# Recurrence heads in two parts, a banded pair that stays on the chip, and gates two ahead: a fused transformer kernel on one core

## The chip, the cores and the metric

The kernel runs on one core of one Trainium2 chip. The metric is the device time of one execution in microseconds (us); the number before is the median of three runs. The engines are named as in the profile: PE is TensorE (matmuls), PEld its weight loads, DVE is VectorE, ACT is ScalarE, POOL is GpSimd, SP is SyncE, which issues the transfers here.

## The reference, cut to what matters

A first block (gated delta mixer, then a convolutional gated feed-forward) is followed by two layers of a second block on 512 positions of width 1024. All of the change lies in the second block:

```python
for l in range(2):
    h = rmsnorm(x, g_mix[l])
    (a_cq, a_ckv, a_kr, b_q, b_ff, b_fb, b_i, b_g, c_q, c_k, c_v,
     gate_a, gate_b, gate_c) = split_cols(h @ w_in[l])
    y_a = mla(a_cq, a_ckv, a_kr, ...)          # low-rank attention, 8 heads
    y_b = hgrn2(b_q, b_ff, b_fb, b_i, b_g, ..) # gated recurrence, 8 heads, forward and backward
    y_c = window_gqa(c_q, c_k, c_v, ...)       # banded attention, 8 heads, blocks of 128
    merged = (sigmoid(gate_a) * (y_a @ w_br_a[l]) + sigmoid(gate_b) * (y_b @ w_br_b[l])
              + sigmoid(gate_c) * (y_c @ w_br_c[l]))
    x = x + merged @ w_out[l]
    x = x + cross(rmsnorm(x, g_x[l]), ...)
    x = x + swiglu(rmsnorm(x, g_ffn[l]), ...)
```

## The kernel before, in words

Everything is fp32, made of products of a rounded high part and a low rest: a matrix product is three matmuls per 128 rows (`mm3`, L158 to L160). A **strip** (`strip`) is one 128-column block of `h @ w_in`: 24 matmuls of 128x512 into one PSUM bank, behind one weight load (SP), one cast to the high part (`cast_hi`, L111, on ACT) and one subtraction for the low part (`sub_lo`, L120, on DVE, on POOL for the early gates). The weights have three raw buffers and two each of high and low parts; strips have three PSUM banks (`psg`), scores and the recurrence's triangles two (`psa`), transposes and states two (`psb`), outputs one (`pso`).

`layer` runs, in the order of the text: `hgrn`, `mla`, `branch` b, `window`, `branch` a, `branch` c, the output projection, `cross`, `ffn`. The text's order isn't the queues' order. A planner plays the program ahead of the run with its own model of times and fills each engine's queue; of the instructions that it holds ready it takes the one that stands first in the text, and `high_priority(100)` moves a block 100 places forward. So an engine runs later work where earlier work isn't ready, as far as buffers allow. What is planned is fixed: on the chip every engine works through its queue in order.

A recurrence head (`hgrn_head`) has two halves. **Strips and gates** (to L1069): three strips (q, forward and backward gate), and for each direction a chain over ACT, DVE and POOL (exponentials, a scan at L1048, products at L1045, L1053, L1054, L1055), then the block decays `XE` (L1062 to L1069). **Products** (from L1071): level and block tiles (L1084, L1095 on DVE and POOL), 16x16 up to 64x64 triangles on PE (L1107 to L1121), transposes (L1129), the state chain (L1148 on PE, L1151 on ACT or L1153 on DVE, six steps in turn in one bank), and the output matmuls (L1158). Even and odd heads have separate pools for the tiles of the gates; the tiles of the products (`hlv`, `hbk`, `hkm`, `hkt`, `hA`) are shared. `hgrn` calls the heads one after the other; at odd heads it first makes the strip of the output gate, and after each head `early_gate` makes one strip of the branch gates with its sigmoid and stores it for later (8 of them here, 8 more in `mla`, which serve branches b and a).

`mla` starts with loads of the rotary tables `cos`, `sin`, `ssin` into its pool `low`, two strips for the key rank and three for the query rank, each followed by a norm, and then, in a block with `high_priority(AHEAD)`, AHEAD being 100, the strip of the rotary key (evacuated at L797 and L798) and the value product (L814 to L816). Its pools lie where those of `hgrn` lay.

`window` works four pairs of heads (s = 0 to 3); each pair's output `Y` goes to DRAM (`keep_y`, L737) and `branch_in` (L1179 to L1181) loads it back (`yl`, L99) and splits it into `ys`. `branch` then makes, for each of eight blocks m, the gate (loaded if early, else a strip and a sigmoid, which holds for branch c alone) and the product of 12 matmuls with the `ys` of its four pairs.

Of the kernel before, what the change touches and what calls it, by code (L numbers as in the profile page):

```python
# [9 lines left out]
F32R = mybir.dt.float32r  # L10
BF16 = mybir.dt.bfloat16
I32 = mybir.dt.int32
AF = mybir.ActivationFunctionType
# [4 lines left out]
P = 128  # L18
# [6 lines left out]
def f32(ap):  # L25
    return ap.bitcast(F32)
# [631 lines left out]
def c2(p, name):  # L658
    o, n = p.cst2_off[name]
    return p.c2[:, o:o + n]  # L660
# [74 lines left out]
def keep_y(p, y, ys):  # L735
    d = p.dram([P, 512], "yd")
    p.nc.sync.dma_start(d, y)  # L737
    ys.append(d)


def side_by_side(p, ps, out, scale=None):
# [16 lines left out]
def mla(p, l, G, low, mid, high):  # L758
# [9 lines left out]
            acc = p.square_add(acc, z[i], i == n - 1)  # L768
        return z, p.rstd_rows(acc, nf)


    cos, sin, ssin = (p.load(p.ins["big"][i], n, 1, pool=low) for n, i in (("cos", 0), ("sin", 1), ("ssin", 2)))
    z, rr = rank(at["ckv"], 2, 256, "za")
    CKV = []
    for i in range(2):
# [5 lines left out]
    nc.vector.tensor_scalar(g, p.col(f"a_gq{l}"), 96 ** -0.5, None, MULT)  # L781
    CQ = [p.split(z[i], "CQ", 6, g[:, i:i + 1], pool=low) for i in range(3)]

    def four():
        t = p.t("s4", 4, 1024)
        return t[:, :512], t[:, 512:]
# [2 lines left out]

    half = (slice(0, 64), slice(64, 128))  # L790
    kh, kl = ([p.t(f"{n}{i}", 1, dtype=F32R) for i in range(2)] for n in ("kh", "kl"))

    V = []
    with p.tc.high_priority(AHEAD):
        ps = p.strip(w_in, at["kr"], p.X)
        a, b = four()
        nc.vector.tensor_tensor(a[:64], ps[:64], cos[:64], MULT)  # L797
        nc.vector.tensor_tensor(b[:64], ps[64:], ssin[:64], MULT)  # L798
        nc.gpsimd.tensor_tensor(a[:64], a[:64], b[:64], ADD)
        nc.gpsimd.tensor_tensor(a[:64], a[:64], p.r[:64], MULT)  # L800
        for i in range(2):
            R = half[1 - i]
            m = c2(p, "keven")[:64, i:i + 1]
            nc.scalar.activation(kh[i][R], a[:64], AF.Identity, scale=m)
            nc.vector.scalar_tensor_tensor(kl[i][R], a[:64], m, f32(kh[i][R]), MULT, SUB)

        wvh, wvl = p.wload(f"w_uv{l}", 0, 1024)
        for t in range(4):
            ps = p.ps()
            ts = slice(t * P, t * P + P)  # L810
            for k in range(2):
                xh, xl = CKV[k]
                c = slice(k * 512, k * 512 + 512)
                nc.tensor.matmul(ps, xh[:, ts], wvh[:, c], start=k == 0, stop=False)  # L814
                nc.tensor.matmul(ps, xh[:, ts], wvl[:, c], start=False, stop=False)
                nc.tensor.matmul(ps, xl[:, ts], wvh[:, c], start=False, stop=k == 1)  # L816
            V.append(side_by_side(p, ps, p.t("V", 4, 1024, F32R)))

    nc.vector.tensor_tensor(cos, cos, rq, MULT)
    nc.gpsimd.tensor_tensor(sin, sin, rq, MULT)  # L820
# [66 lines left out]
def window(p, l, G):  # L887
    nc = p.nc
    at = G.at
    w_in = f"w_in{l}"  # L890
    half = [slice(0, 64), slice(64, 128)]


    k = strip_r(p, w_in, at["ck"])
    K = []
    for kv in range(2):
        kh, kl = p.t("K", 2, dtype=F32R), p.t("Kl", 2, dtype=F32R)
        for i in range(2):
            nc.scalar.activation(kh[half[i]], k[half[kv]], AF.Copy)
        nc.vector.tensor_tensor(kl[half[kv]], k[half[kv]], f32(kh[half[kv]]), SUB)  # L900
        nc.gpsimd.memset(f32(kl[half[1 - kv]]), 0.0)
        K.append((kh, kl))
    v = strip_r(p, w_in, at["cv"])
    pv = p.ps("b")
    for t in range(4):
        nc.tensor.transpose(pv[:, t * P:t * P + P], v[:, t * P:t * P + P], p.ident)

    V = []
    for kv in range(2):
        t = p.t("V", 2)  # L910
        c = lambda a, i: a.rearrange("p (t i c) -> p t i c", t=4, i=2)[:, :, i]
        nc.scalar.copy(c(t, kv), c(pv, kv))
        nc.gpsimd.memset(c(t, 1 - kv), 0.0)
        V.append(t)
    for s in range(4):
        q = strip_r(p, w_in, at["cq2"] + s)
        O = p.ps("o")
        Y = p.t("x", 3, keep=True)
        T = {}
        for kv in range(2):  # L920
            h = s + 4 * kv
            R = slice(kv * 64, kv * 64 + 64)
            qq = p.t("Q", 8, dtype=F32R)
            nc.scalar.activation(qq[R], q[R], AF.Copy)
            nc.gpsimd.tensor_tensor(qq[half[1 - kv]], q[R], f32(qq[R]), SUB)
            kh, kl = K[kv]
            sink = p.col(f"sink{l}")[:, h:h + 1]
            wb = window_bias_head(p, h)
            negm, den, es = (p.small([P, 4], n, 3) for n in ("w4m", "w4d", "w4e"))
            E = []  # L930
            for qb in range(4):
                k0, k1 = max(qb - 1, 0), min(qb + 2, 4)
                W = (k1 - k0) * P
                qs = slice(qb * P, qb * P + P)
                ks = slice(k0 * P, k1 * P)
                sc = p.ps("a")[:, :W]
                nc.tensor.matmul(sc, qq[:, qs], kh[:, ks], start=True, stop=False)
                nc.tensor.matmul(sc, qq[:, qs], kl[:, ks], start=False, stop=True)
                sb = p.t("wsb", 10, 384)[:, :W]
                off = (k0 - qb + 1) * P  # L940
                nc.vector.tensor_tensor_reduce(sb, sc, wb[:, off:off + W], 0.125, sink, ADD, MAX,
                                               accum_out=negm[:, qb:qb + 1])
                nc.vector.tensor_scalar(negm[:, qb:qb + 1], negm[:, qb:qb + 1], -1.0, None, MULT)
                nc.scalar.activation(sb, sb, AF.Exp, bias=negm[:, qb:qb + 1], accum_out=den[:, qb:qb + 1])
                E.append(sb)
            nc.scalar.activation(es, negm, AF.Exp, bias=sink)
            nc.vector.tensor_tensor(den, den, es, ADD)
            nc.vector.reciprocal(den, den)
            for qb in range(4):
                k0, k1 = max(qb - 1, 0), min(qb + 2, 4)  # L950
                W = (k1 - k0) * P
                qs = slice(qb * P, qb * P + P)
                nc.vector.tensor_scalar(E[qb], E[qb], den[:, qb:qb + 1], None, MULT)
                pt = p.ps("b")[:, :W]
                for kb in range(k1 - k0):
                    nc.tensor.transpose(pt[:, kb * P:kb * P + P], E[qb][:, kb * P:kb * P + P], p.ident)
                pts = p.t("pts", 8, 384)[:, :W]
                nc.scalar.copy(pts, pt)
                T[kv, qb] = pts
                if kv == 1:  # L960
                    for i in range(2):
                        for kb in range(k0, k1):
                            nc.tensor.matmul(O[:, qs], V[i][:, kb * P:kb * P + P],
                                             T[i, qb][:, (kb - k0) * P:(kb - k0) * P + P],
                                             start=i == 0 and kb == k0, stop=i == 1 and kb == k1 - 1)
        nc.scalar.copy(Y, O)
        keep_y(p, Y, G.y["c"])

# [13 lines left out]
def hgrn(p, l, G, pools, tail):  # L984
# [8 lines left out]
    for t in range(4):  # L993
        V.append(p.t("Vb", 4))
        nc.scalar.activation(V[t], pst[t], AF.Identity, scale=p.rc[:, t:t + 1])
    for h in range(8):
        if h % 2 == 0:
            O = p.ps("o")
        else:
            z = strip_r(p, w_in, at["bg"] + h // 2)  # L1000
            a = p.sigmoid(z, p.t("za", 3, keep=True))
            nc.gpsimd.tensor_tensor(a, z, a, MULT)
        hgrn_head(p, l, G, h, V, O[(h % 2) * 64:(h % 2) * 64 + 64], pools[h % 2])
        early_gate(p, l, G)
        if h % 2 == 1:
            o = p.t("x", 3, keep=True)
# [8 lines left out]
            keep_y(p, o, G.y["b"])  # L1015


def hgrn_head(p, l, G, h, V, O, pool):

    nc = p.nc  # L1020
    w_in, b0 = f"w_in{l}", G.at[f"b{h}"]
# [45 lines left out]
    nc.scalar.activation(dec, XE[:, 2].rearrange("p d (t c) -> p d t c", c=8)[:, :, :, 7], AF.Exp, scale=-1.0)  # L1067
    nc.vector.tensor_tensor(flat(XE), flat(XE), Tb, SUB)
    nc.scalar.activation(XE, XE, AF.Exp, scale=-1.0)  # L1069

    D = [p.ps("a"), p.ps("a")]  # L1071

# [82 lines left out]
    for t in range(4):  # L1155
        parts = [(V[t][:, hv], A[:, ts(t)])] + [(S[d][t], Q128[d](t)) for d in range(2) if t in S[d]]
        for i, (w, x) in enumerate(parts):
            mm(O[:, ts(t)], w, x, start=i == 0, stop=i == len(parts) - 1)  # L1158

# [16 lines left out]

def branch_in(p, G, pool, n):  # L1179

    return [p.split(p.load(d, "yl", 2, pool=pool), "ys", 8, le="g", pool=pool) for d in G.y[n]]  # L1181


def branch(p, l, G, n, Y):

    nc = p.nc
    bi = "abc".index(n)
    M = []
    for m in range(8):
        if (bi, m) in G.early:  # L1190
            a = p.load(G.early[bi, m], "za", 3, keep=True)
        else:
            z = strip_r(p, f"w_in{l}", G.at[f"g{m}"] + bi)
            a = p.sigmoid(z, p.t("za", 3, keep=True))
        pb = p.ps()
        p.gemm_block(pb, p.wload(f"w_br_{n}{l}", m, 512), Y, P, 0, 4)
        if G.acc[m] is None:
# [132 lines left out]
MULT, ADD, SUB, MAX, MIN = ALU.mult, ALU.add, ALU.subtract, ALU.max, ALU.min  # L1330

SCP = 60
AHEAD = 100
GS, MORE, RB, F0, F1, FP = [[0], [1], [2, 3]], 2, 8, 32, 4.6, 10
NT = 6
L0 = 258
# [866 lines left out]
```

## Time and profile before

| | us |
|---|---|
| median of 3 runs | 3630.03 |
| lowest, highest of the 3 | 3628.92, 3635.11 |
| the profiled execution's own time | 3632.3 |
| its span from first to last instruction | 3630.5 |

| engine | busy us | share of the span |
|---|---|---|
| PE | 3432.1 | 95% |
| PEld | 2835.4 | 78% |
| DVE | 2288.7 | 63% |
| ACT | 1718.2 | 47% |
| POOL | 1215.7 | 33% |

Times in the trace count from the first instruction. In layer 0 the heads of the recurrence run from about 1160 to 1470, the start of the low-rank attention to about 1545, and the banded attention ends at about 1780; in layer 1 these places are 2400 to 2705, 2785 and 3025. The granted clock is given as a share of the higher of TensorE's two levels, 2.4 GHz; at the lower one, 1.2 GHz, it is half. A busy PE counts a matmul at either level, so time lost to the lower level hides in the busy time and is read from the clock's column. The mean granted clock of the execution is 0.969.

### The profile page before, as it was taken

The numbers are of one execution on the slowest core, as the hardware profiler recorded it, in microseconds if no ns is written. First come the engines' busy times: TensorE is split into PE (matmuls) and PEld (weight loads), VectorE is DVE, ScalarE is ACT, GpSimd is POOL, SyncE is SP. The second block draws the span as 40 slices with busy tenths as digits, with TensorE's granted clock in tenths as the row PEclk, the third lists the DMA queues.
The fourth block names the chain that finished last, engine by engine and source line by source line (L and its number), as shares of the span: only waits on it lengthen the run. The fifth ranks groups of instructions, "written<-read, shape, count | busy, mean of one in ns | idle before, by whom it ended". The sixth has DMA issues, their size and how long they took to land.

```text
span 3630.5 us, 51931 instructions
## 1 busy us (share of the span) xinstructions
PE 3432.1 (95%) x19472; PEld 2835.4 (78%) x19472; DVE 2288.7 (63%) x3613; ACT 1718.2 (47%) x3125; POOL 1215.7 (33%) x1166
## 2 busy tenths in 40 slices
PE   7999789999999999899999999999988999999998
PEld 5877789878888777688778888877776887778886
DVE  6877776755534777686566665357776865656643
ACT  5776454344433444375544444234444755444431
POOL 3576774322211434233121221124443331212221
PEclk8999889999999999899999999999999999999999
DMA  5346675443333222134253333421222442533332
GB/s 193 104 106 188 200 225 177 149 142 93 99 114 121 73 73 73 61 114 139 83 163 102 110 99 102 127 92 67 76 69 72 126 125 86 158 116 94 98 102 90
DMA packets 239612, 417.84 MB, mean 115 GB/s; under 512 B 78464, under 2 KB 121728, under 8 KB 239360
## 3 DMA queue, kind: packets, MB, share of 16 engines
q1 hardware_dynamic: 239360, 414.52, 36.6%
q8 instruction: 154, 2.52, 0.3%
q14 instruction: 98, 0.80, 0.1%
HBM read 355.97 MB, written 56.36 MB: 114 GB/s over the span
## 4 chain that ended last, share of the span: by engine, by line
PE 53%; DVE 7%; ACT 2%; POOL 2%; issue 2%; DMA 1%; DVEq 0%; SPq 0%; POOLq 0%; ACTq 0%
PE ffn_psg L159 4%; PE ffn_psg L160 4%; PE ffn_psg L158 4%; PE f_psg L160 2%; PE f_psg L159 2%; PE f_psg L158 2%; PE br_psg L159 2%; PE br_psg L160 2%; PE br_psg L158 2%; PE hg_psg L160 1%; PE hg_psg L159 1%; PE hg_psg L158 1%; PE eg_psg L160 1%; PE eg_psg L159 1%; PE eg_psg L158 1%
## 5 line engine op out<-in xcount | busy, mean ns | idle before, releaser
L160 PE MATMUL ffn_psg<-xo_X,ffn_wl 128*128 128x512 f32 x704 | 274.7, 390 | 0.0
L159 PE MATMUL ffn_psg<-xo_X,ffn_wh 128*128 128x512 f32 x704 | 273.9, 389 | 0.0
L158 PE MATMUL ffn_psg<-xo_X,ffn_wh 128*128 128x512 f32 x704 | 273.9, 389 | 0.0
L120 DVE TENSOR_TENSOR ffn_wl<-ffn_wr,ffn_wh 128x1024 fp32r<-128x1024 f32 x88 | 153.5, 1745 | 19.7 <-ACT ffn_wh L111 19.7
L158 PEld LDWEIGHTS ffn_psg<-xo_X,ffn_wh 128*128 128x128 f32 x704 | 132.2, 188 | 28.1 <-issue 0.5
L159 PEld LDWEIGHTS ffn_psg<-xo_X,ffn_wh 128*128 128x128 f32 x704 | 132.2, 188 | 27.7
L160 PEld LDWEIGHTS ffn_psg<-xo_X,ffn_wl 128*128 128x128 f32 x704 | 132.2, 188 | 27.5 <-issue 0.5
L724 DVE TENSOR_TENSOR ffn_z<-ffn_psg,xo_ry 128x512 f32<-128x512 f32 x88 | 60.6, 691 | 142.9 <-PE ffn_psg L160 142.7
L1270 POOL TENSOR_TENSOR ffn_z<-ffn_z,ffn_z 128x512 f32<-128x512 f32 x44 | 57.3, 1302 | 274.4 <-DVE ffn_z L724 233.9
L120 POOL TENSOR_TENSOR eg_wl<-eg_wr,eg_wh 128x1024 fp32r<-128x1024 f32 x32 | 78.0, 2443 | 189.7 <-ACT eg_wh L111 176.6
L160 PE MATMUL f_psg<-ffn_U,f_wl 128*128 128x512 f32 x352 | 140.8, 400 | 0.0
L159 PE MATMUL glu_psg<-gout_X,glu_wh 128*128 128x512 f32 x352 | 137.7, 392 | 3.1 <-DVE gout_X L1428 3.1
L158 PE MATMUL glu_psg<-gout_X,glu_wh 128*128 128x512 f32 x352 | 137.9, 392 | 1.9 <-ACT gout_X L1427 1.9
L159 PE MATMUL f_psg<-ffn_U,f_wh 128*128 128x512 f32 x352 | 138.7, 394 | 0.0
L120 DVE TENSOR_TENSOR f_wl<-f_wr,f_wh 128x1024 fp32r<-128x1024 f32 (+1 forms) x48 | 56.8, 1183 | 129.3 <-ACT f_wh L111 129.3
L158 PE MATMUL f_psg<-ffn_U,f_wh 128*128 128x512 f32 x352 | 138.0, 392 | 0.0
L160 PE MATMUL glu_psg<-gout_X,glu_wl 128*128 128x512 f32 x352 | 137.7, 391 | 0.0
L111 ACT ACTIVATE ffn_wh<-ffn_wr 128x1024 fp32r<-128x1024 f32 x88 | 93.6, 1064 | 92.2 <-PE ffn_psg L159 67.5
L111 ACT ACTIVATE f_wh<-f_wr 128x1024 fp32r<-128x1024 f32 (+1 forms) x48 | 47.5, 990 | 167.3 <-PE f_psg L159 139.8
L120 DVE TENSOR_TENSOR glu_wl<-glu_wr,glu_wh 128x1024 fp32r<-128x1024 f32 x44 | 56.4, 1282 | 101.6 <-ACT glu_wh L111 101.3
L120 DVE TENSOR_TENSOR hg_wl<-hg_wr,hg_wh 128x1024 fp32r<-128x1024 f32 x64 | 87.2, 1362 | 33.7 <-ACT hg_wh L111 33.5
L111 ACT ACTIVATE hg_wh<-hg_wr 128x1024 fp32r<-128x1024 f32 x64 | 67.5, 1054 | 62.1 <-PE hg_psg L159 28.7
(870 smaller groups left out, 11421.2 us busy)
## 6 DMA issues: line engine op xcount, KB each, us to landing
ffn_wr<-in_f_w_dram SPq DMA_DIRECT2D x88, 512.0 KB, 3.4
hg_wr<-in_w_in_dram SPq DMA_DIRECT2D x56, 512.0 KB, 3.4
glu_wr<-in_ffn_in_dram SPq DMA_DIRECT2D x44, 512.0 KB, 3.5
fill_C<-in_w_mod_dram SPq DMA_DIRECT2D x64, 256.0 KB, 4.6
eg_wr<-in_w_in_dram SPq DMA_DIRECT2D x32, 512.0 KB, 3.4
f_wr<-in_f_w_dram SPq DMA_DIRECT2D x32, 512.0 KB, 3.6
prep_wr<-in_gdn_in_dram SPq DMA_DIRECT2D x24, 512.0 KB, 3.7
mod_wm<-in_w_mods_dram SPq DMA_DIRECT2D x16, 512.0 KB, 10.2
```

The lines of the kernel that those rows point to most:

```text
L111: nc.scalar.activation(hi, src, AF.Copy)
L120: e.tensor_tensor(lo, src, f32(hi), ALU.subtract)
L158: nc.tensor.matmul(ps, wh, xh, start=start, stop=False)
L159: nc.tensor.matmul(ps, wh, xl, start=False, stop=False)
L160: nc.tensor.matmul(ps, wl, xh, start=False, stop=stop)
L724: p.nc.vector.tensor_tensor(t, ps, p.r, MULT)
L1270: nc.gpsimd.tensor_tensor(z1, z1, z3, MULT)
```

## The change

- `hgrn_head` becomes a generator that stops after the strips and gates. `hgrn` runs the first half of head 0, and then, for each head h, the first half of head h+1, the output gate's strip (odd h), the products of head h, and the early gate.
- In `mla` the block with `high_priority` goes: the rotary key's strip and the value product stand where they are in the text, at no raised priority. The three rotary tables are loaded after the query rank, into the pool `mid` in place of `low`.
- The last pair of `window` isn't stored: its `Y` is handed to `branch_in` in SBUF, which splits it there.
- `branch` asks for gates 0 and 1 ahead of its loop, and in step m for gate m+2 ahead of the product of m. This holds for loaded gates and for those of branch c, which are strips.

```diff
 def keep_y(p, y, ys):
     d = p.dram([P, 512], "yd")
     p.nc.sync.dma_start(d, y)
-    ys.append(d)
+    ys.append((d, None))
...
-    cos, sin, ssin = (p.load(p.ins["big"][i], n, 1, pool=low) for n, i in (("cos", 0), ("sin", 1), ("ssin", 2)))
     z, rr = rank(at["ckv"], 2, 256, "za")
...
     CQ = [p.split(z[i], "CQ", 6, g[:, i:i + 1], pool=low) for i in range(3)]
 
+    cos, sin, ssin = (p.load(p.ins["big"][i], n, 1, pool=mid) for n, i in (("cos", 0), ("sin", 1), ("ssin", 2)))
...
+    ps = p.strip(w_in, at["kr"], p.X)
+    a, b = four()
+    nc.vector.tensor_tensor(a[:64], ps[:64], cos[:64], MULT)
...
+    wvh, wvl = p.wload(f"w_uv{l}", 0, 1024)
     V = []
-    with p.tc.high_priority(AHEAD):
-        ps = p.strip(w_in, at["kr"], p.X)
-        a, b = four()
-        nc.vector.tensor_tensor(a[:64], ps[:64], cos[:64], MULT)
...
-        wvh, wvl = p.wload(f"w_uv{l}", 0, 1024)
...
         nc.scalar.copy(Y, O)
-        keep_y(p, Y, G.y["c"])
+        if s < 3:
+            keep_y(p, Y, G.y["c"])
+        else:
+            G.y["c"].append((None, Y))
...
+    heads = [hgrn_head(p, l, G, h, V, pools[h % 2]) for h in range(8)]
+    next(heads[0])
     for h in range(8):
+        if h < 7:
+            next(heads[h + 1])
         if h % 2 == 0:
             O = p.ps("o")
...
-        hgrn_head(p, l, G, h, V, O[(h % 2) * 64:(h % 2) * 64 + 64], pools[h % 2])
+        heads[h].send(O[(h % 2) * 64:(h % 2) * 64 + 64])
         early_gate(p, l, G)
...
-def hgrn_head(p, l, G, h, V, O, pool):
+def hgrn_head(p, l, G, h, V, pool):
...
     nc.scalar.activation(XE, XE, AF.Exp, scale=-1.0)
+    O = yield
...
-    return [p.split(p.load(d, "yl", 2, pool=pool), "ys", 8, le="g", pool=pool) for d in G.y[n]]
+    return [p.split(Y if d is None else p.load(d, "yl", 2, pool=pool), "ys", 8, le="g", pool=pool) for d, Y in G.y[n]]
...
-    M = []
-    for m in range(8):
+    A, M = [], []
+
+    def gate(m):
         if (bi, m) in G.early:
-            a = p.load(G.early[bi, m], "za", 3, keep=True)
+            A.append(p.load(G.early[bi, m], "za", 3, keep=True))
         else:
             z = strip_r(p, f"w_in{l}", G.at[f"g{m}"] + bi)
-            a = p.sigmoid(z, p.t("za", 3, keep=True))
+            A.append(p.sigmoid(z, p.t("za", 3, keep=True)))
+
+
+    gate(0), gate(1)
+    for m in range(8):
+        if m + 2 < 8:
+            gate(m + 2)
+        a = A[m]
```

## Rows read from the trace of the kernel before

**Rows 1.** The page: busy time, then the granted clock in 40 slices (tenths).

```profile
PE 3432.1 (95%) x19472; PEld 2835.4 (78%) x19472; DVE 2288.7 (63%) x3613; ACT 1718.2 (47%) x3125; POOL 1215.7 (33%) x1166
...
PEclk8999889999999999899999999999999999999999
```

**Rows 2.** Busy time by stretch: heads, attention's start, banded end, both layers.

```profile
core 0: us, PE busy (x) PEld busy (x) DVE busy (x) ACT busy (x) POOL busy (x), PEclk, DMA share, GB/s
1160.00:1470.00 310.00, 290.91 (x2134) 239.72 (x2133) 221.55 (x284) 142.81 (x256) 123.36 (x97) 0.96 0.24 75
1470.00:1545.00 75.00, 61.12 (x300) 47.20 (x299) 44.21 (x68) 26.06 (x45) 18.58 (x14) 0.89 0.19 59
1760.00:1790.00 30.00, 21.59 (x135) 18.69 (x133) 9.61 (x36) 14.12 (x38) 2.54 (x2) 0.88 0.17 53
2400.00:2705.00 305.00, 275.75 (x2041) 226.48 (x2040) 221.49 (x274) 145.42 (x261) 138.69 (x106) 0.96 0.22 73
2705.00:2785.00 80.00, 66.33 (x353) 51.34 (x353) 52.93 (x76) 28.63 (x50) 23.09 (x19) 0.89 0.17 57
3005.00:3035.00 30.00, 21.57 (x135) 18.30 (x134) 10.97 (x36) 13.66 (x35) 4.66 (x3) 0.89 0.17 53
```

**Rows 3.** Waits of PE, 1160 to 1470: us in total, times, longest.

```profile
PE hg_psa L1121 <- DVE hg_hlv L1084: 4.8, 4, 2.6
PE hg_psa L1107 <- DVE hg_hl L1053: 3.4, 1, 3.4
```

**Rows 4.** Waits of PE, 2400 to 2705.

```profile
PE hg_psb L1148 <- ACT hg_hst L1151: 7.9, 2, 5.8
PE hg_pso L1158 <- DVE hg_hst L1153: 7.7, 2, 5.1
```

**Rows 5.** Waits of PE, 1470 to 1545.

```profile
PE mla_psg L814 <- DVE mla_s L798: 6.0, 1, 6.0
```

**Rows 6.** Waits of PE, 1760 to 1790.

```profile
PE br_psg L158 <- ACT br_ys L111: 6.1, 1, 6.1
PE win_psb L956 <- DVE win_wsb L953: 2.2, 1, 2.2
```

**Rows 7.** Chain that ended last, 1770 to 1792: start us, us, what.

```profile
1781.29 1.99 DMA win_yd<-win_x
...
1783.41 2.60 DMA br_yl<-win_yd
...
1786.03 0.64 ACT br_ys L111
```

**Rows 8.** Timeline of PE at the banded end: start us, us, line, what.

```profile
1758.80 0.39 PE L159 MATMUL br_psg<-gl_X,br_wh 128*128 128x512 f32 x1
1759.03 0.39 PE L160 MATMUL br_psg<-gl_X,br_wl 128*128 128x512 f32 x1
...
1789.09 0.63 PE L159 MATMUL br_psg<-br_ys,br_wh 128*128 128x512 f32 x1
1789.51 0.63 PE L160 MATMUL br_psg<-br_ys,br_wl 128*128 128x512 f32 x1
```

**Rows 9.** Timeline of SP at the attention's start, layer 0.

```profile
1499.89 0.38 SPq L99 DMA_DIRECT2D mla_cos<-in_big_dram  x1
```

**Rows 10.** Timeline of PE, products of layer 0's last head.

```profile
1504.19 0.49 PE L1129 MATMUL hg_psb<-cstt,hg_hbk 128*128 128x128 f32 x3
...
1515.03 0.63 PE L1158 MATMUL hg_pso<-hg_hbk,hg_hst 128*64 128x128 f32 x2
```

**Rows 11.** Timelines of DVE and then of POOL in head 0's gates.

```profile
1173.79 2.20 DVE L1035 TENSOR_SCALAR hg_hz<-hg_hz 128x512 f32<-128x512 f32 x1 [0.70 <-ACT hg_hz L1034]
...
1182.27 0.42 DVE L1035 TENSOR_SCALAR hg_hz<-hg_hz 128x512 f32<-128x512 f32 x1
...
1173.31 2.39 POOL L120 TENSOR_TENSOR eg_wl<-eg_wr,eg_wh 128x1024 fp32r<-128x1024 f32 x1 [38.21 <-ACT eg_wh L111]
1177.49 1.30 POOL L1045 TENSOR_TENSOR hg_ha<-hg_hz,hg_ha 128x512 f32<-128x512 f32 x1 [1.78 <-ACT hg_ha L1038]
```

More of the change, by code (lines that the diff above doesn't have):

```diff
@@ L791, in mla @@
     kh, kl = ([p.t(f"{n}{i}", 1, dtype=F32R) for i in range(2)] for n in ("kh", "kl"))
-    V = []
-    with p.tc.high_priority(AHEAD):
-        ps = p.strip(w_in, at["kr"], p.X)
-        a, b = four()
-        nc.vector.tensor_tensor(a[:64], ps[:64], cos[:64], MULT)
[L798 to L805, printed above, removed]
-        wvh, wvl = p.wload(f"w_uv{l}", 0, 1024)
[L808 to L817, printed above, removed]
@@ new lines, in mla @@
+    ps = p.strip(w_in, at["kr"], p.X)
+    a, b = four()
+    nc.vector.tensor_tensor(a[:64], ps[:64], cos[:64], MULT)
+    nc.vector.tensor_tensor(b[:64], ps[64:], ssin[:64], MULT)
+    nc.gpsimd.tensor_tensor(a[:64], a[:64], b[:64], ADD)
+    nc.gpsimd.tensor_tensor(a[:64], a[:64], p.r[:64], MULT)
+    for i in range(2):
+        R = half[1 - i]
+        m = c2(p, "keven")[:64, i:i + 1]
+        nc.scalar.activation(kh[i][R], a[:64], AF.Identity, scale=m)
+        nc.vector.scalar_tensor_tensor(kl[i][R], a[:64], m, f32(kh[i][R]), MULT, SUB)
@@ new lines, in mla @@
+    wvh, wvl = p.wload(f"w_uv{l}", 0, 1024)
+    V = []
+    for t in range(4):
+        ps = p.ps()
+        ts = slice(t * P, t * P + P)
+        for k in range(2):
+            xh, xl = CKV[k]
+            c = slice(k * 512, k * 512 + 512)
+            nc.tensor.matmul(ps, xh[:, ts], wvh[:, c], start=k == 0, stop=False)
+            nc.tensor.matmul(ps, xh[:, ts], wvl[:, c], start=False, stop=False)
+            nc.tensor.matmul(ps, xl[:, ts], wvh[:, c], start=False, stop=k == 1)
+        V.append(side_by_side(p, ps, p.t("V", 4, 1024, F32R)))
@@ L1158, in hgrn_head @@
             mm(O[:, ts(t)], w, x, start=i == 0, stop=i == len(parts) - 1)
+    yield
 def early_gate(p, l, G):
@@ L1332 @@
 SCP = 60
-AHEAD = 100
 GS, MORE, RB, F0, F1, FP = [[0], [1], [2, 3]], 2, 8, 32, 4.6, 10
```

## The prediction

> **What bounds the kernel now.** I read the page first: PE is busy for 3432.1 us, 95% of the span, and the granted clock stands at 9 tenths or more in nearly every slice [rows 1]. Nothing else comes near, so time can be won only where PE stands still, and where it runs at the lower level, 1.2 GHz, behind such a stop. Next I asked for busy time by stretch, for the three places that the change touches, in both layers [rows 2]. The reader is to see two numbers in each row, the length less PE's busy time, and the clock's column. Idle PE: heads 310.0 - 290.9 = 19.1 and 305.0 - 275.8 = 29.2; attention's start 13.9 and 13.7; banded end 8.4 and 8.4; together 92.7 us. The clock's column gives (1 - clock) times the length as what the lower level takes: 12.4 and 12.2; 8.3 and 8.8; 3.6 and 3.3; together 48.6 us. These two overlap where the clock is low while PE stands still, so at most some 125 us can be won in all, and a part of it only. Third come the waits of PE in each stretch, which say what each stop waits for [rows 3 to 6]: in the heads the product tiles and the state chain, at the attention's start one wait of 6.0 us, at the banded end one of 6.1 and one of 2.2. DVE is busy for 221.5 of 310 us in the heads: it is full in bursts and not on the mean.
>
> **The change part by part.** No matmul is added or taken away; what counts is what is ready for PE when it would stop.
>
> Banded end, per layer. A store of 1.99 us and a load of 2.60 us lie one behind the other in the chain that ends in the wait of 6.1 us [rows 6, 7]; both go, and with the issues around them the chain is shorter by 1786.03 - 1781.29 = 4.7 us. Nothing is queued behind the two on SP that this would delay. Left are the cast of 0.64 us and the hop to PE [rows 7]. The second part is work to put in the hole. In the row before the stop PE ends its last strip for a gate of branch c at 1759.03 and then has none [rows 8], though six of the eight are still to be made: I read it so that the two pairs of weight buffers are held by the products that wait for the band. With gates asked for two ahead, three strips stand ahead of the first product, one more than now. A strip is 24 matmuls at 0.23 us, the distance of two starts in [rows 8], so 5.5 us. Needed after the shorter chain: 2.2 + (6.1 - 4.7) = 3.6 us, so it covers the rest. I take 8 of the 8.4 us idle, and 1 of the 3.6 of the clock, which shows as starts 0.42 apart in place of 0.23 behind the stop [rows 8]. That is 9 per layer, 18 us for both; bounds 2 x 4.7 = 9 (the strip doesn't get there) and 2 x 12 = 24 (stop and slow clock gone). For branches b and a the two ahead are loads: each stands two steps earlier in SP's queue, behind it a weight load of the branch. A load costs 2.60 us [rows 7]; if the wait for its buffer held up the weights in all 8 steps of both branches, that would be 42 us per layer. I take 0, the other end, because the order among loads is planned and weights have three raw buffers, and leave this to the upper end of the range.
>
> Attention's start, per layer: 13.8 idle and about 8.5 of clock. Products of the last head run here alone: from its first transpose at 1504.19 to its last output at 1515.03 take 10.8 us [rows 10], in which PE does little else, because the strips of the attention have been run earlier, under the gates of heads 6 and 7. In the new order the gates of head 7 lie beside the products of head 6, so these strips are left to cover the products of head 7. I take half of the 10.8 us, 5.4. The stop of 6.0 us behind L798 is a strip that was raised, holds one of three banks, and can't be evacuated until DVE is done with the last head's tail [rows 5]; at its place in the text it comes three strips (16 us) later. I take half of it, 3.0; the bounds are 0 and 6.0. The reverse price of losing the raised priority is that the key strip and its chain come late for the scores; nothing shows it, and the nearest row is the same 6.0 us, so -6.0. The three table loads move behind the query rank; in the trace the first is issued at 1499.89, behind all but the last strips anyway [rows 9], so I count nothing, covered by the strip under way, and 2.60 us for a load that isn't covered. With the clock I take 9 per layer, 18 us; bounds -6 x 2 = -12 and 2 x 18 = 36.
>
> Heads, per layer: idle 24 on the mean and 12 of clock. Stops lie where products wait for tiles from DVE and POOL that come right behind the gates of the same head [rows 3], and, in layer 1, in the state chain behind DVE and ACT at their fullest [rows 4]. A whole head of distance between gates and products takes the first kind away. The second stays in part: product tiles are shared by all heads, so products of two heads still follow one another. I take 10 per layer, a bit over a quarter, 20 us; bounds +30 per layer, and below nothing: products that now stand behind the next head's strips can be left without cover. Its price is the 10.8 us stretch less the PE work in it, about half, so 5.4 us for each of 14 heads, -76 us in all.
>
> Sum: 18 + 18 + 20 = 56 us from 3632.3, the profiled execution's own time (its span is 3630.5, so 1.8 us lie around it): 3576. The median of the runs is 2.3 us less, so 3574.
>
> **A rule against it.** In head 0 one minimum on DVE takes 2.20 us and its twin 0.42 us; the long one starts at 1173.79 while POOL works from 1173.31 to 1175.70, and ends just behind that [rows 11]. The Trainium skill, page "SBUF — State Buffer", section "Who interferes with whom", has it that DVE and GpSimd share one pair of ports and that the later of the two is fully blocked until the first is done. By that, laying one head's gates beside another's products lengthens DVE's work, and the 20 us of the heads would be lost; the trace agrees as far as this one pair shows.
>
> **The rivals.** *Products uncovered* (slower). The next head's strips go first, and the products of a head, with the state chain of six steps, run when only an early gate's strip (5.5 us) is left. For it: the 10.8 us of the last head [rows 10] show what that looks like. Against it: per head there are an early strip, half an output gate's strip and the first two strips of the next but one, 5.5 + 2.7 + 11 = 19 us, more than 10.8. It decides if less than some 11 us of strips stay to be issued in a head's products. Half of the 76 us, no gain in the heads, and the other 36 halved: 3630 + 38 + 5 - 18 = 3655; in full, 3688.
>
> *Port and burst.* POOL has four gate products per head in layer 0, six in layer 1, of 1.30 us [rows 11]; if each held up DVE for its length, DVE would have 8 x 4 x 1.30 = 42 us more in layer 0 and 62 in layer 1: 221.5 + 42 = 263 of 291 and 221.5 + 62 = 284, above the 276 of PE. So DVE gets full in layer 1, the heads gain nothing, and 3630 - 36 = 3594 is left.
>
> *The planner had it already.* It was free to run later work early, and does [rows 8]; the text's order then changes little in heads and attention, a raised block is lost, and only the shorter chain counts: 9 us less, against up to 12 more at the attention's start. That gives 3621 to 3633, say 3627, no change.
>
> **How the numbers follow.** Forecast (gain of 25 to 100 us): 0.61. Port and burst, or a like gain of 8 to 50: 0.13. Planner had it: 0.11. Products uncovered: 0.15. The measurement of this kernel can tell some 0.2%, 7.3 us, from no change. Faster: 0.61 + 0.13 = 0.74; same 0.11; slower 0.15. The low end takes the upper bounds of the banded end and the attention's start and two thirds of the heads': 24 + 36 + 40 = 100, 3530. The high end takes in "same" and the start of "uncovered", 3640. Left out are some 0.10 above and 0.07 below.
>
> **What would show it.** Banded end: no store and load behind the last output, the wait of 6.1 us for `ys` gone, three strips of `br` gates ahead of the first product. Attention's start: the wait behind L798 below 3 us, clock above 0.95. Heads: strips of head h+1 ahead of the triangles of head h, PE's waits for L1084 gone, and those for L1151 and L1153 fewer; PE idle below 15 us in layer 0 and 20 in layer 1. Wrong would be me if waits at L1148 and L1158 grow to several us per head (uncovered), or DVE's time in the heads grows by tens of us (port).

## The result and the profile after

The changed kernel takes 3594.3 us (median of four runs, 3592.1 to 3596.1) against 3630.9 for the kernel before on the same chip: 0.9892 of it, 95% interval 0.9879 to 0.9904. Forecast were 3574 and a gain of 56 us from the profiled execution; measured are 40 between the profiled executions (3632.3 and 3592.1) and 37 between the medians. Two rows of the page, busy time and clock, which answer [rows 1]:

```profile
PE 3416.6 (95%) x19472; PEld 2819.6 (79%) x19472; DVE 2305.5 (64%) x3613; ACT 1719.0 (48%) x3125; POOL 1233.8 (34%) x1166
...
PEclk8999889999999999899999999999998999999999
```

To see where the time went I divide the second block at tiles that both kernels write: the first `Vb` of the recurrence, the first and last score, the first and last output projection. Groups by tile, before (three rows) and after (three rows); the last two numbers are the first and last start:

```profile
L995 ACT ACTIVATE hg_Vb<-hg_psa,fin_rq x2: 688/689/690, 1158.1 to 1159.3; 128x512 f32<-128x512 f32 x2
L158 PE MATMUL mla_psa<-mla_kh,mla_qh x64: 387/397/481, 1543.1 to 2902.0; 128*128 128x512 f32 x64
L158 PE MATMUL wo_psg<-br_M,wo_wh x128: 392/394/500, 1841.2 to 3129.3; 128*128 128x512 f32 x128
```
```profile
L996 ACT ACTIVATE hg_Vb<-hg_psa,fin_rq x2: 688/689/690, 1158.2 to 1159.3; 128x512 f32<-128x512 f32 x2
L158 PE MATMUL mla_psa<-mla_kh,mla_qh x64: 387/397/481, 1525.4 to 2868.3; 128*128 128x512 f32 x64
L158 PE MATMUL wo_psg<-br_M,wo_wh x128: 388/394/399, 1814.8 to 3088.6; 128*128 128x512 f32 x128
```

The differences of these starts are the stages of the next table; every later kernel is read in the same way. H0 runs from the first `Vb` to the first score (heads and attention's start of layer 0), B0 from there to the first output projection (with its banded end), H1 to the last score (with the heads of layer 1), B1 to the last output projection. "Ratio" is to the kernel before on the same chip; the kernels ran on more than one chip, so two kernels are compared by their ratios. The stages come from one profiled execution of each kernel. One of e7's four runs took 11706.5 us, which is in its median and not in its ratio.

| kernel | H0 | B0 | H1 | B1 | median | ratio (95%) |
|---|---|---|---|---|---|---|
| before | 385.0 | 298.1 | 1060.8 | 227.3 | 3630.9 | |
| after | 367.2 | 289.4 | 1053.5 | 220.3 | 3594.3 | 0.9892 (0.9879 to 0.9904) |
| e1 banded end alone | 384.9 | 289.7 | 1057.0 | 220.0 | 3614.6 | 0.9951 (0.9936 to 0.9965) |
| e2 heads alone | 373.7 | 297.0 | 1049.7 | 228.1 | 3610.2 | 0.9938 (0.9924 to 0.9953) |
| e3 attention alone | 384.4 | 297.1 | 1060.1 | 228.1 | 3629.9 | 0.9994 (0.9985 to 1.0003) |
| e4 after, old attention | 375.6 | 289.4 | 1049.2 | 219.9 | 3594.8 | 0.9895 (0.9878 to 0.9911) |
| e5 no DRAM alone | 384.8 | 293.3 | 1060.2 | 224.0 | 3624.0 | 0.9973 (0.9963 to 0.9982) |
| e6 gates ahead alone | 385.3 | 294.3 | 1059.3 | 224.6 | 3624.7 | 0.9975 (0.9964 to 0.9986) |
| e7 after, key tile | 367.0 | 289.5 | 1053.6 | 221.6 | 3597.1 | 0.9899 (0.9879 to 0.9919) |
| e8 after, no subtraction | 367.7 | 289.5 | 1042.8 | 220.4 | 3585.6 | 0.9867 (0.9852 to 0.9881) |
| e9 after, V's banks | 364.8 | 289.8 | 1050.3 | 219.9 | 3588.5 | 0.9882 (0.9867 to 0.9896) |
| e10 after, subtraction on DVE | 367.4 | 289.6 | 1053.4 | 219.9 | 3591.6 | 0.9888 (0.9874 to 0.9903) |
| e11 e9 and e10 | 368.9 | 289.7 | 1050.3 | 220.3 | 3591.6 | 0.9888 (0.9873 to 0.9903) |
| e12 e9, e10 and e7 | 363.7 | 292.8 | 1050.6 | 220.2 | 3589.3 | 0.9882 (0.9866 to 0.9899) |

After gains 17.8 + 8.7 + 7.3 + 7.0 = 40.8 us. Busy time by stretch after, as [rows 2] has it before: heads, attention's start and banded end of layer 0, then of layer 1:

```profile
1160.00:1452.00 292.00, 279.60 (x2123) 228.91 (x2122) 218.85 (x280) 139.91 (x255) 120.05 (x90) 0.99 0.25 80
1452.00:1527.00 75.00, 60.31 (x308) 46.10 (x308) 47.20 (x71) 27.77 (x48) 25.14 (x20) 0.89 0.19 58
1749.00:1779.00 30.00, 26.38 (x163) 21.88 (x162) 15.03 (x35) 14.93 (x36) 6.07 (x4) 1.00 0.17 54
2372.00:2672.00 300.00, 278.86 (x2088) 228.77 (x2087) 228.82 (x275) 148.22 (x265) 149.03 (x106) 0.96 0.23 76
2672.00:2752.00 80.00, 64.34 (x308) 48.42 (x307) 51.51 (x74) 26.61 (x47) 22.33 (x19) 0.83 0.16 51
2980.00:3010.00 30.00, 27.33 (x149) 22.13 (x149) 14.14 (x30) 14.17 (x32) 6.06 (x4) 0.94 0.20 63
```

Length less PE's busy time gives idle 12.4 and 21.1 us in the heads (19.1 and 29.2 before), 3.6 and 2.7 at the banded ends (8.4 each), but 14.7 and 15.7 at attention's start (13.9 and 13.7 before), where the clock is 0.89 in layer 0, as before, and 0.83 in layer 1, lower than the 0.89 before. PE's waits say the same: the longest of layer 0's heads, of its attention's start and banded end, then of layer 1's heads.

```profile
PE hg_psb L1155 <- DVE hg_hst L1160: 2.0, 3, 1.2
...
PE mla_psg L812 <- DVE mla_s L795: 6.6, 1, 6.6
...
PE br_psg L158 <- ACT br_ys L111: 1.3, 1, 1.3
...
PE hg_psb L1155 <- ACT hg_hst L1158: 4.5, 1, 4.5
PE hg_psg L160 <- DVE hg_wl L120: 3.2, 2, 2.9
PE hg_psb L1155 <- DVE hg_hst L1160: 2.9, 3, 1.6
PE hg_pso L1165 <- DVE hg_hst L1160: 2.9, 1, 2.9
PE hg_psa L1128 <- POOL hg_hlv L1091: 2.5, 2, 2.2
```

The wait of 6.1 for the band's `ys` [rows 6] has become 1.3. The wait of 6.0 for the key strip [rows 5] stands there as 6.6: what was to shrink at attention's start has not.

### The profile page after: what moved, and what is told of

The parts are those of the page before. It is cut to its first block, busy times and chain, and to the rows that moved or that the text cites. A ratio compares the mean times of both kernels' runs of the same rounds, so it can differ in the third digit from the quotient of the medians.

```text
span 3590.2 us, 51915 instructions
## 1 busy us (share of the span) xinstructions
PE 3416.6 (95%) x19472; PEld 2819.6 (79%) x19472; DVE 2305.5 (64%) x3613; ACT 1719.0 (48%) x3125; POOL 1233.8 (34%) x1166
## 4 chain that ended last, share of the span: by engine, by line
PE 73%; DVE 13%; POOL 5%; ACT 4%; issue 3%; DMA 2%; SPq 1%; DVEq 0%; POOLq 0%; ACTq 0%
PE ffn_psg L159 4%; PE ffn_psg L160 4%; PE ffn_psg L158 4%; PE f_psg L160 2%; PE f_psg L159 2%; PE f_psg L158 2%; PE glu_psg L159 2%; PE glu_psg L160 2%; PE glu_psg L158 2%; PE br_psg L160 2%; PE br_psg L159 2%; PE br_psg L158 2%; PE hg_psg L160 1%; PE hg_psg L159 1%; PE hg_psg L158 1%
```

## The experiments

**Which part gives what.** Theory A: the parts add, and attention's edit is worth nothing. Rivals: heads and attention need one another (C), or attention's edit costs in layer 1 (D).

*e1*, the diff's parts in `keep_y`, `window`, `branch_in` and `branch` alone:

> Kernel before with the banded end of the change alone: the last pair's output stays in SBUF and the branch's gates are computed two ahead; heads and attention's start as before. Theory A (the three parts add, each where it stands): the two banded ends gain 8.7 and 7.0 us as they do in the trace of the changed kernel, so 3615, 15.7 below before; the heads' idle time stays at 19 and 29 us. Rival B (part of those 15.7 us comes from the heads' new order shifting loads and clock): 3619 to 3624.

*e2*, the diff's parts in `hgrn` and `hgrn_head` alone:

> Kernel before with the split of the recurrence heads alone; attention's start and the banded end as before. Theory A (the attention edit is worth about nothing): the heads gain 17.5 us in layer 0 and about 8 in layer 1, so 3605 to 3609. Rival C (the heads gain only because the keys and V products of attention were taken out of their way): less than half, 3618 to 3624, and the attention edit alone gains the rest.

*e3*, the diff's part in `mla` alone:

> Kernel before with the attention edit alone: the key strip and V products lose their priority, the tables are loaded after the ranks into another pool. Theory A: the wait of the V products behind the key strip's evacuation stays near 6 us in both layers, and the time is within 4 us of before (3627 to 3635). The forecast on record: 18 us gained (3613). Rival C: 10 us or more gained, in the heads.

*e4*, the whole change without the diff's part in `mla`:

> The changed kernel with attention's start as before (priority and early tables put back). Theory A: within 4 us of the changed kernel (3590 to 3598), the V products' wait about 6 us as in both kernels. Rival C: it loses 10 us or more (3604 and above), in the heads' stretch. Rival D (the edit costs in layer 1, where the clock at attention's start fell from 0.89 to 0.83): 3 to 8 us faster, 3586 to 3591.

By the ratios e1 gains 17.8 us of 3632, e2 22.5 and e3 2.2 (its interval takes in no change), together 42.5 against 39.2 for the whole: within these intervals the parts add. A's times hold for e1, e3 and e4; e2's 3610.2 is 1.2 above A's 3605 to 3609. The stages say more. The heads alone gain 11.3 us in H0 and 11.1 in H1, not 17.5 and 8 as theory A had it. Attention's edit alone moves H0 and H1 by 0.6 and 0.7. Beside the split, after against e4, H0 is 8.4 shorter and H1 4.3 longer. So there is something of C in layer 0 (the heads gain without attention's edit, but that edit gains beside them alone) and of D in layer 1, and the total hides both: by the ratios after and e4 are 1.1 us apart. The same 2431 or 2432 matmuls stand in H0 of both; whole H0 of after, then of e4:

```profile
1158.20:1525.40 367.20, 340.11 (x2431) 275.20 (x2430) 265.79 (x352) 168.59 (x303) 143.59 (x109) 0.97 0.23 75
```
```profile
1157.60:1533.20 375.60, 345.84 (x2432) 280.58 (x2431) 265.09 (x352) 168.78 (x303) 142.42 (x109) 0.95 0.23 74
```

Idle differs by 29.8 - 27.1 = 2.7 us, PE's busy time by 5.7: what differs is clock rather than waits, and the wait behind the key strip is 6.1 in e4 and 6.6 in after. Not all of the 8.4 is the edit's. Up to 1469 in after the four engines have the same instructions in the same order in both kernels, and yet e4 is 2.8 us behind by 1442, since PE was granted the lower level (1.2 GHz) for longer there. For example, the same 6.8 us counted from the first `Vb`, 25 matmuls in after and 14 in e4:

```profile
1216.80:1223.60 6.80, 5.78 (x25) 4.36 (x25) 6.80 (x11) 3.21 (x6) 3.37 (x4) 1.00 0.29 80
```
```profile
1216.20:1223.00 6.80, 5.92 (x14) 4.50 (x14) 6.80 (x11) 3.03 (x5) 3.42 (x4) 0.50 0.20 80
```

The other 5.6 lie at attention's start. There e4 has, against 14.7 idle and 0.89 in after, 17.8 idle and 0.85:

```profile
1452.00:1533.00 81.00, 63.22 (x313) 49.12 (x312) 47.28 (x73) 27.78 (x50) 22.23 (x19) 0.85 0.16 52
```

The signs stand in other kernels too. H0 is 373.7 and 375.6 without attention's edit (e2, e4) and 367.0 to 367.7 with it (after, e7, e8, e10); H1 is 1049.7 and 1049.2 without it, 1053.5 and 1053.6 with it (after, e7). So the edit is worth some 6 us in layer 0 and costs some 4 in layer 1. That attention's start of layer 1 runs at 0.83 in after is a row; why it does was not settled.

**The banded end's two edits.**

*e5*, without the diff's part in `branch`; *e6*, with that part alone:

> Kernel before with the last banded pair kept in SBUF, the branch's gates in their old order. The trace of before has PE waiting 6.1 us for this pair; its store and load took 1.99 and 2.60 us. Theory A (the two edits of the banded end cover the same wait): the wait falls by 4.6 to some 1.5 us in each layer and with the clock 9 to 12 us are gained of the 17.5 that both gave, 3620 to 3623. Rival B (they add, each its own wait): 5 us or less, 3627.

> Kernel before with the branch's gates two ahead, the last pair still over DRAM. Theory A: two more strips (some 8 us of matmuls at full clock) stand in front of the first product, longer than the wait of 6.1 us, so that they hide it alone: 13 to 17 us gained, 3615 to 3619, and with the other run more than the 17.5 us of both. Rival B: less than 10 us, 3622 and above, because the strips' own weights come too late.

They gain 9.8 and 9.1 us by the ratios, 18.9 together against e1's 17.8; in B0 and B1 together 8.1 and 6.5, against 15.7. They add, each with its own wait, as rival B had it. The size of e5 is theory A's, 9 to 12, not B's 5 or less. That of e6 is B's, under 10, but not for B's reason: no wait for the strips' weights stands among its waits. PE's waits at the banded end, of e5 and then of e6:

```profile
PE win_psb L956 <- DVE win_wsb L953: 2.2, 1, 2.2
PE br_psg L158 <- ACT br_ys L111: 1.3, 1, 1.3
```
```profile
PE br_psg L158 <- ACT br_ys L111: 6.0, 1, 6.0
```

Without the DRAM trip the wait for `ys` falls to 1.3, and the older wait of 2.2 inside the band stays. With the gates ahead it is the other way round: the 2.2 is gone and the 6.0 stands. The planner does not keep the extra strips for the hole behind the last pair; it runs them beside the band's softmax, where PE was starved too. In after four strips, not three, stand ahead of that hole; the last of them ends by 1760.5, and the product that waits starts at 1771.4.

**Why attention's start did not gain.** DVE's timeline in after shows it; start, length, line:

```profile
1495.02 0.28 DVE L1160 SCALAR_TENSOR_TENSOR hg_hst<-hg_hst,hg_hdc,hg_psb 128x64 f32<-128x64 f32 x1 [0.79 <-PE hg_psb L1155]
1502.66 0.69 DVE L229 TENSOR_SCALAR hg_hrm<-hg_psb 128x512 f32<-128x512 f32 x1 [7.36 <-ACT hg_hry L228]
...
1506.43 0.69 DVE L1020 TENSOR_TENSOR hg_x<-hg_x,hg_za 128x512 f32<-128x512 f32 x1
1507.04 0.68 DVE L794 TENSOR_TENSOR mla_s<-mla_psg,mla_cos 64x512 f32<-64x512 f32 x1
1507.74 0.69 DVE L795 TENSOR_TENSOR mla_s<-mla_psg,mla_ssin 64x512 f32<-64x512 f32 x1
```

The key strip's matmuls end before 1477, but its evacuation (L794, L795) stands in DVE's queue behind the last head's normalisation (L229 to L1020). DVE stands still for 7.36 us ahead of that, since the normalisation needs the last head's outputs. Key strip and two V blocks hold all three `psg` banks meanwhile.

*e7* gives the evacuation memory of its own:

```diff
-    a, b = four()
+    a, b = p.t("za", 3, keep=True), p.t("z", 3, keep=True)
```

> The changed kernel; the key strip is evacuated into two tiles of the pool that lives through all stages, in place of the tile s4, which lies over the last head's products hbk. Theory M (that memory is what kept the evacuation behind the last head's outputs, and so behind its tail on DVE): the evacuation runs some 8 us earlier, the third V product is no longer stopped, the wait of 6.6 us falls to below 4 (the fourth product can still wait for a bank, since V's own evacuations stay behind the tail), and 4 to 12 us are gained over both layers, 3582 to 3590. Rival O (the order of DVE follows the text, memory has no part): wait and time stay, 3592 to 3597.

```profile
1498.92 0.68 DVE L794 TENSOR_TENSOR mla_za<-mla_psg,mla_cos 64x512 f32<-64x512 f32 x1
```
```profile
PE mla_psg L812 <- DVE mla_V L749: 6.1, 1, 6.1
```

Counted from the first `Vb`, which comes 3.0 us later in e7, the evacuation runs 11 us earlier, as theory M had it, and the time stays, as rival O had it (H0 367.0, H1 1053.6): now the fourth V block waits 6.1 us for V's own evacuation, which is still behind the normalisation. The tile did matter to DVE's order, since the edit changes nothing else, but not as the expectation had it. In the compiled layout `s4` lies over `hbk` only in the kernel before; since the split it lies over the gates' `ha` and `hl`, and V's tiles lie over the products. How the evacuation then comes to stand behind the last head's tail stays open.

*e9* takes two V blocks off `psg`:

```diff
-        ps = p.ps()
+        ps = p.ps("a") if t < 2 else p.ps()
```

> The changed kernel; the first two V products of attention go to the two banks of scores and triangles (psa) in place of psg, so that key strip and V together need three psg banks no longer. Theory B (PE stops because key strip and two V blocks hold all three psg banks while their evacuations stand on ACT and DVE behind the last head's normalisation): all four V blocks run beside the last head's products; the stop moves to the query products behind them and stays near 6 us, since they too need a psg bank, but the 12 V matmuls that ran behind it (1508.5 to 1513.5 in layer 0) are out of the way: 4 to 6 us per layer, 3582 to 3587. Rival S (V's products only lengthen the last head's state chain between them): within 3 us of the changed kernel, 3591 to 3597.

All V blocks now run beside the last head, and the stop, 6.59 us, stands in front of the query products, as theory B had it. But with 12 matmuls out of the way H0 is 2.4 us shorter and H1 3.2, not 4 to 6 each, and 3588.5 lies between the times of B and of S. (The 3.2 comes again in e11 and e12 below; the 2.4 does not come again in e11.) Windows of the stop, of the time behind it at the lower clock and of that at the full one, after (first fence) and e9:

```profile
1495.00:1508.40 13.40, 5.21 (x20) 4.00 (x20) 5.74 (x9) 3.50 (x6) 0.00 (x0) 0.63 0.03 12
1508.40:1513.40 5.00, 4.91 (x12) 3.87 (x13) 3.02 (x6) 1.86 (x3) 2.89 (x2) 0.54 0.07 25
1513.40:1519.90 6.50, 6.50 (x29) 5.25 (x28) 5.44 (x9) 1.71 (x5) 1.32 (x2) 1.00 0.27 81
```
```profile
1497.00:1510.40 13.40, 5.14 (x22) 3.93 (x22) 5.78 (x9) 4.48 (x8) 1.26 (x1) 0.64 0.25 97
1510.40:1514.70 4.30, 4.26 (x10) 3.37 (x11) 3.56 (x6) 1.20 (x2) 2.90 (x2) 0.52 0.05 20
1514.70:1518.90 4.20, 4.20 (x19) 3.38 (x18) 4.17 (x7) 0.89 (x3) 1.28 (x2) 1.00 0.00 0
```

In after the V blocks were what ran at half clock behind the stop (0.54); in e9 the query products take that place (0.52), so their 27 matmuls need 8.3 us in place of 6.3: 2.0 of the 4.9 us are given back. What was pulled forward had been cheap cover for the slow clock.

**Why layer 1's heads kept 21 us idle.** Theory P: GpSimd's work beside DVE lengthens DVE's. Rival S: it is the state chain.

*e8* and *e10*, layer 1's subtraction left out, and put on DVE (the edit shown is e10's; e8 has no line in its place):

```diff
-            nc.gpsimd.tensor_tensor(u, u, v, SUB)
+            nc.vector.tensor_tensor(u, u, v, SUB)
```

> The changed kernel without the subtraction L1050 of layer 1's gates (GpSimd, 16 of 1.48 us); left out is one term of the gate's logarithm, so layer 1's values differ. Theory P (GpSimd's work lengthens DVE's beside it): in layer 1's heads the DVE scan L1054 falls from 1.68 to about 1.3 us and the weights' low parts from 1.44 to 1.3, PE's waits for the low parts shrink, idle falls from 21 towards layer 0's 12, and 6 to 12 us are gained, 3582 to 3588. Rival S (PE's idle time there is the state chain, PE to DVE or ACT and back, whatever GpSimd does): DVE gets shorter, but the time stays within 3 us, 3591 to 3597.

> The changed kernel with layer 1's subtraction L1050 on DVE in place of GpSimd (16 of some 0.7 us there against 1.48). Theory P (GpSimd lengthens DVE beside it): the scan L1054 falls from 1.68 to near 1.3 us as it did with the subtraction left out; DVE's busy time in the heads of layer 1 stays at about 229 us (11 more, 10 saved), and of the 9 us that leaving it out gave, 4 to 9 are kept: 3586 to 3591. Rival D (DVE is the engine that sets the pace in layer 1, so that what is added to it costs in full): 3594 to 3603.

The scan of layer 1's gates by tile, minimum, median and longest ns, in before, after and e8:

```profile
L1048 DVE TENSOR_TENSOR_SCAN hg_hz<-set_c,hg_hl x16: 1209/1214/2300, 2416.5 to 2701.1; 128x512 f32<-128x512 f32 x16
```
```profile
L1054 DVE TENSOR_TENSOR_SCAN hg_hz<-set_c,hg_hl x16: 1203/1225/3387, 2388.1 to 2654.3; 128x512 f32<-128x512 f32 x16
```
```profile
L1053 DVE TENSOR_TENSOR_SCAN hg_hz<-set_c,hg_hl x16: 1209/1212/2303, 2386.6 to 2646.4; 128x512 f32<-128x512 f32 x16
```

The split itself made this: the median is one and the same, but after has long ones among the 16 (mean 1.68 us, against 1.28 before and in e8). Without the subtraction H1 is 10.7 us shorter (9.1 for the whole, by the ratios) and PE's idle time in the heads falls from 21.1 to 290.0 - 273.7 = 16.3. P's time holds; its 12 us of idle does not, and PE's waits for ACT's states are 7.2 us in e8, so S keeps a part. e8 also shortens the gates' chain by one step, which it doesn't tell apart from the contention. e10 keeps that step. DVE (third number) from layer 1's first `Vb` to its last score, in after, e8 and e10:

```profile
2365.40:2868.30 502.90, 466.04 (x3038) 381.26 (x3037) 377.75 (x530) 258.31 (x480) 215.30 (x150) 0.95 0.26 83
```
```profile
2366.20:2858.70 492.50, 461.05 (x3039) 378.62 (x3038) 366.59 (x530) 258.60 (x480) 184.62 (x134) 0.96 0.26 85
```
```profile
2365.20:2868.40 503.20, 467.63 (x3039) 381.89 (x3038) 385.27 (x546) 258.69 (x480) 188.32 (x134) 0.95 0.26 83
```

The 16 subtractions take 1.11 us each on DVE, 17.7 together, and not the 0.7 each of the expectation. The other 530 instructions then take 385.3 - 17.7 = 367.6 us, near the 366.6 of e8 and 10 below after. So the subtraction on GpSimd did lengthen DVE's work by some 10 us, though the scan gets only a part of them back (its mean falls from 1.68 to 1.54). But in e10 DVE's load is 7.5 us greater in all, and H1 stays (1053.4). The median of 3591.6 lies between P's 3586 to 3591 and D's 3594 to 3603 and is not told from after's. D is not shown either, as the 7.5 us cost nothing. Whether e8's 10.7 us come from the load taken off DVE or from the step taken out of the chain stays open.

**Together.**

> The changed kernel with both of the last two edits: V's first two products on other banks, layer 1's subtraction on DVE. They act in different stretches (attention's start, layer 1's heads), so they should add: 3574 to 3582. If they only move the same idle time, 3583 or more.

> As the run before, and the key strip evacuated into tiles that do not lie over the last head's memory. With V on other banks an early evacuation of the key strip frees a psg bank for the query products, which alone needed both: theory B then gives up to 3 us per layer more, 3570 to 3579; if the second bank that they need is freed no earlier, the time of the run before within 3 us.

They do not add: e11's H1 is that of e9 alone (1050.3), as e10's edit is worth nothing. Its H0 is 4.1 us longer than e9's, though PE, DVE, ACT and GpSimd have the same instructions in the same order there. H0 of e9, then of e11:

```profile
1159.60:1524.40 364.80, 339.27 (x2431) 274.58 (x2430) 265.70 (x352) 168.39 (x303) 143.16 (x109) 0.98 0.24 76
```
```profile
1162.40:1531.30 368.90, 343.62 (x2432) 277.43 (x2431) 266.23 (x352) 168.47 (x303) 143.21 (x109) 0.96 0.24 75
```

Idle is 25.5 and 25.3, PE's busy time 4.4 apart, the clock 0.98 and 0.96: the granted clock alone moved this stage by 4 us between two executions that have the same queues there. Why it was granted otherwise no run shows. So e9's 2.4 us in H0 is not shown to be a gain; its 3.2 in H1 is there in e11 and e12 too (1050.3, 1050.6). In e12 the stop in layer 0 is 4.4 us in place of 6.6, and the time is within 3 us of e11's, the second case of its expectation; H0 is 1.1 below e9's, less than the clock can move it, and B0 is 3.0 longer, with another order of the queues. e9 has the lowest median of the kernels that compute the whole, 0.8 under e12's. By the ratios it is 3.6 us under after, but their intervals overlap, so it is faster than before for certain and than after only by H1.

## Why the prediction came out as it did

The range held the time and the sign was right; the sum was 16 to 19 us too large.

- *Banded end, 18 forecast.* Right in size: 15.7 in the stages, 17.8 alone. Its division was wrong. The step that failed is "it covers the rest": e6's wait of 6.0 shows that strips ahead of the product don't go into that hole. The shorter chain alone took the wait to 1.3 and gave the lower bound, 9 (9.8 measured); the gates gave as much, elsewhere. If loads two ahead held up anything, it was less than they gave: B0 and B1 are shorter in e6.
- *Heads, 20 forecast.* e2 gives 11.3 and 11.1, each close to the 10 taken. The waits behind `hlv` of layer 0 [rows 3] are no longer among the longest, and those of the states in layer 1 [rows 4] are 4.5, 2.9 and 2.9, from 7.9, 7.7 and 5.0 (the 5.0 is L1148 behind DVE's states, which [rows 4] leaves out), as reasoned. The clock in layer 0's heads rose from 0.96 to 0.99. Of the signs given, idle below 15 in layer 0 came (12.4), below 20 in layer 1 did not (21.1).
- *Attention's start, 18 forecast.* This is the term that failed: against the kernel before, idle and clock there gained nothing. Two steps were wrong. First, strips "left to cover the products of head 7": the planner still ran them earlier, the key strip's by 1477, and the last head's products, from 1484.70 to 1499.44, have 12 matmuls of V beside them and no strip. Secondly, a later key strip was taken to shorten the stop. The bank is freed by the evacuation, which stands behind the last head's normalisation in both kernels. Neither sign came: the wait is 6.6 and not below 3, the clock 0.89 and 0.83 and not above 0.95. What the edit was worth beside the split, some 6 us in layer 0 and some -4 in layer 1, lies within the bounds given. In layer 0 it took back what the split had cost this stretch: without it (e4) idle was 17.8 and the clock 0.85, against 13.9 and 0.89 before.
- *The rivals.* Products uncovered: waits on the state chain fell from 20.6 to 10.3 us in layer 1's heads and went from 1.7 to 3.3 in layer 0's, far from several us per head, so no. Planner had it: the heads gained, so no. Port and burst gave 3594, the measured number, but by a mechanism that didn't happen: the heads' gain was to be lost and attention's kept, and e2 and e3 show the reverse. That the measured number is there is luck. In small the mechanism is there too: in layer 1 DVE's busy time rose by 5.4 us for the same 530 instructions from the first `Vb` to the last score (372.4 to 377.8), not by 62, and in layer 0, over H0, by 0.3.
- *The arithmetic.* Two numbers come from no row: the 5 us in the sum for uncovered products, and the step from 92.7 + 48.6 = 141 to "some 125 us". The forecast uses neither.

## What to carry to other kernels

Before a stop is counted as won, find what frees the buffer that it waits for, and where that instruction stands in its engine's queue: moving the producer changes nothing if the consumer stays behind the same tail. Extra work "for a hole" goes where a planner first has room, so count it as cover for the whole stage, and test two edits to one place apart. A part that costs or gives nothing in the total can be two effects of opposite sign, so divide the trace into stages at tiles that both kernels write. Then look at the granted clock before a stage's few us are called a gain: here it moved a stage by 4 us between two executions of the same queues.

## What the runs showed of the hardware

A DVE scan of 1.2 us took 3.39 us while GpSimd subtracted weights (after, layer 1; DVE, then POOL):

```profile
2443.67 3.39 DVE L1054 TENSOR_TENSOR_SCAN hg_hz<-set_c,hg_hl 128x512 f32<-128x512 f32 x1
```
```profile
2443.43 2.54 POOL L120 TENSOR_TENSOR eg_wl<-eg_wr,eg_wh 128x1024 fp32r<-128x1024 f32 x1
```

They overlap for 2445.97 - 2443.67 = 2.30 us, and 3.39 - 2.30 = 1.09, nearly the scan's own 1.2: DVE did next to nothing until GpSimd had ended. The Trainium skill, "SBUF — State Buffer", section "Who interferes with whom", says that a DVE instruction with two SBUF inputs contends with a GpSimd instruction that reads SBUF, and that for the shared pair of ports the later one is fully blocked; this pair agrees.

Behind the stop of 6.6 us PE ran for 4 to 5 us at 0.52 to 0.54 of its clock, the lower level (1.2 GHz), and then at 1.00, the full one (2.4 GHz), whether V blocks (after) or query products (e9) stood there. I had counted a strip's length as its gain when it is moved ahead of such a stop; in e9's layer 0 the 12 matmuls moved had taken 4.9 us, and 2.0 of them came back.

The same instructions in the same order got different clocks in two executions: 0.98 in H0 of e9 and 0.96 in H0 of e11, which is 4.1 us.
